# Chunk matrices in other PSUM banks, waits for both banks of a run, and a second block-diagonal tile, in a hybrid RWKV-7 and attention step

## The chip, the cores and the metric

One core of a Trainium2 chip runs one layer of a hybrid decoder as a single program. The metric is the time of one execution on the device, in microseconds (us). Engine names are those of the profile: PE is TensorE's matmul, PEld its weight load, DVE is VectorE, ACT ScalarE, POOL GpSimd, SP the engine that issues most of the DMAs.

## The reference, cut to what matters

One prompt of 4096 tokens and a sample batch of 8 x 8 tokens go through one layer of width 1024. A joint projection feeds eight RWKV heads and eight windowed attention heads; both outputs are gated, projected and added to the input. The part that the change touches is the recurrence of the RWKV heads:

```python
def step(S, xs):
    r_t, w_t, k_t, v_t, a_t, b_t = xs
    Sa = jnp.einsum('bhvk,bhk->bhv', S, a_t)
    S = S * w_t[:, :, None, :] + Sa[..., None] * b_t[:, :, None, :] + v_t[..., None] * k_t[:, :, None, :]
    return S, jnp.einsum('bhvk,bhk->bhv', S, r_t)
```

The kernel doesn't step through tokens. It takes chunks of 64 tokens, for which the recurrence becomes products of 64 x 64 matrices and the inverse of a triangular one.

## The kernel before, in words

The first phase (`phase1`) projects the input and runs the recurrence; the second (`phase_b`) does the attention and the output projections. The prompt is cut into 16 supertiles of 256 tokens (four chunks each); the sample is a 17th, taken second. Per supertile there are four pairs of heads (units); two units make a group, so there are 34 groups.

Stages of the first phase, for the reader of the rows:

- Stage B (`stage_b`): the projections that the recurrence needs, `g_ps` (lines 592 to 594); `shift` copies them out as `k`, `r`, `v` (line 607).
- Stage W (`stage_w`): the other projections, `w_ps` (line 683), with weights streamed from memory; their results go back to memory for the second phase.
- Stage C (`stage_c`, one unit): decay and keys, to the operands `AR` (lines 777 and 798) and `BK` (lines 780 and 801), the bonus `bo` (line 813) and the values `UV` (line 834). Its small products `sum_ps`, `nb_ps`, `b_ps`, `v_ps` and those of the decay (`dec`, lines 643 and 644) use the PSUM pool `pm`, with two banks.
- Stage D (`stage_d`, one group): `tmat` (line 872), once a unit, makes the chunk matrices `t_ps` in two banks, from which six instructions of VectorE take `nf`, `LA` and `Ar` (lines 882 to 885). `m0` (line 893) puts them into the block-diagonal tile `mbd` and makes the first `DG`. Then the inverse is built level by level: `lev1`, four times `levz` and `levd` (two banks at once), a last `levz`, `lastd`, `nz` (the last to read `mbd`), `lastg` and `ng`, which ends in the copy to `G` (line 994). All of these products use the pool `pi`, with two banks, `tmat` too. Between them `tmt` (line 905) transposes `BK` into a bank of `pm`.
- Stage E (`stage_e`, one group): the four chunks one after the other, with the state; from `mean` (line 1120) on the norm of the output, which ends in `yc` (line 1151) and the store to `y_d` by SP (line 1155).

`BK` has three buffers, `AR` five, `UV` and other tiles of a group three (groups), `TM`, `LA` and `Ar` four, `mbd` one. The sum of all of this must fit the eight banks of PSUM and the on-chip memory.

What sets the order: `Timeline` gives every step a due time (a supertile is 4 units of time; stage D of a group starts 1.05 behind stage C of its second unit, stage E 3.1), and the steps are written down in that order. From there a planner fixes, when the program is built, the order of each engine's instructions and the buffer of each tile: it takes the earliest written step among those whose operands and buffers are ready in its model, stages D and E by some instructions ahead of their place. A tile's buffer is whichever of its pool is free first. `together` (line 181) keeps a run of matmuls in its order; with `after` its first one waits for given instructions (`follow`, line 191):

```python
    def together(calls, after=()):
        for i, (out, lhs, rhs) in enumerate(calls):
            ins = pe.matmul(out, lhs, rhs, start=True, stop=True)
            follow(ins, i, after)
```

The way into the second phase: the output of the last group is stored to `y_d` by SP; behind that store on SP stand the loads of `y_d`, of `z_d` and of `w_proj` (lines 1334, 1338, 1314), and TensorE's first output projection is `g_ps` of line 1636. The tiles `prep` and `parts` of the pool `wsl` (two buffers each) hold weights while they are converted and scaled, up to plan time 19; the sample's attention in the second phase uses them again.

Of the kernel before, what the change touches and what calls it, by code (L numbers as in the profile page):

```python
# [137 lines left out]
def hybrid_step(ctx: ExitStack, tc: tile.TileContext, I, O):  # L138
# [240 lines left out]
    def phase1():  # L379
        with ExitStack() as es:  # L380
# [29 lines left out]
            mbd = ck.tile([128, 2, GN * 4, 128], F16, name="mbd")  # L410
            pool.memset(mbd, 0.0)
# [207 lines left out]
            def stage_b(j):  # L619
# [20 lines left out]
                def dec(p):  # L640
# [9 lines left out]
                    act.activation(th, ps, AF.Tanh, scale=0.5, bias=dcol(13 + p))  # L650
                    ta = sb.tile([128, SUP], F32, tag="ta", name="ta")[:, :n]
                    act.activation(ta, ps2, AF.Tanh, scale=0.5, bias=dcol(17 + p))
# [59 lines left out]
            def stage_c(u):  # L712
# [71 lines left out]
                def s5():  # L784
# [8 lines left out]
                    vec.scalar_tensor_tensor(d["k"], d["k"], vcol(V_KK + p), ps[:, :n], ALU.mult, ALU.mult)  # L793
# [10 lines left out]
                def s8():  # L804
# [5 lines left out]
                    for q in range(2):  # L810
                        os_ = slice(64 - 64 * q, 128 - 64 * q)
                        for h in range(min(nch, 2)):
                            act.activation(bo[os_, h::2], pb[64 * h:64 * h + 64, :nh, q], AF.Copy)
# [3 lines left out]
                def s9():  # L817
# [13 lines left out]
                    for q in range(2):  # L831
                        os_ = slice(64 - 64 * q, 128 - 64 * q)
                        for r in range(min(nch, 2)):
                            act.activation(UV[os_, r:nch:2, q, :],
                                                      ps[64 * r:64 * r + 64, :nh, 64 * q:64 * q + 64], AF.Copy)
# [3 lines left out]
            HALF = [slice(0, 64), slice(64, 128)]  # L839

            def stage_d(g):
# [17 lines left out]
                def with_states(e):  # L859
# [7 lines left out]
                    act.activation(AR[:, 2].rearrange("p i (b t) -> p b i t", t=8), ps, AF.Copy)  # L867
# [4 lines left out]
                def tmat(i):  # L872

                    e = ds[i]
                    pss = [pi.tile([128, 4, 128], F32, tag="i", name="t_ps") for q in range(2)]
                    together([(pss[q][:, c, :], e["BK"][qs, c].rearrange("p a t -> p (a t)"),
                               e["AR"][qs, c].rearrange("p a t -> p (a t)"))
                              for c in range(nch) for q, qs in reversed(list(enumerate(HALF)))], e["w_ab"])
                    mk_ = mlrs if smp else mlr
                    for q, qs in enumerate(HALF):  # L880
# [4 lines left out]
                        vec.tensor_tensor(e["Ar"][:, q, :nch], ps[:, :nch, 64:128], bcm(mk_[:, 64:128], nch), ALU.mult)  # L885
# [7 lines left out]
                def m0():  # L893
                    Nf = d["Nf"][:, :nb]
                    M = d["M"] = mbd[:, :, :nb]
                    for q, hs in enumerate(HALF):
                        own = slice(64 * q, 64 * q + 64)
                        act.activation(M[hs, 0, :, own], Nf[hs], AF.Copy)
                        vec.tensor_tensor(M[hs, 1, :, own], Nf[hs], M[hs, 0, :, own], ALU.subtract)
                    DG = sb.tile([128, 2, GN * 4, 64], F16, tag="DG", name="DG", bufs=2)[:, :, :nb]  # L900
# [4 lines left out]
                def tmt(e):  # L905
# [4 lines left out]
                    act.activation(e["TM"][:, :nch].rearrange("p c q f -> p c (q f)"), ps[:, :nch], AF.Copy)  # L910
# [7 lines left out]
                def mmd(ps, part, rhs):  # L918
                    together([(ps[:, m, :], d["M"][:, part, m], rhs(m)) for m in range(nb)])
# [16 lines left out]
                def lev1():  # L936
                    ps = psn()
                    mmd(ps, 0, lambda m: eye16)
                    vec.tensor_tensor(d["DG"][:, 0], ps, bcm(msk[1], nb), ALU.mult)
                L.append((0.6, lev1))  # L940

                def levz(b):
# [3 lines left out]
                    vec.tensor_tensor(Z, ps, bcm(msk[b], nb), ALU.mult)  # L946
                    d["Z"] = Z

                def levd(b):
# [13 lines left out]
                def lastd():  # L963
# [3 lines left out]
                    act.activation(d["D6"], ps, AF.Copy)  # L967
                L.append((0.6, lastd))

                def nz():  # L970
                    ps = psn()
                    for m in range(nb):
                        for part in range(2):
                            follow(pe.matmul(ps[:, m, :], d["M"][:, part, m], d["D6"][:, m], start=part == 0,
                                             stop=part == 1), 2 * m + part)
                    Zf = sb.tile([128, GN * 4, 64], F32, tag="Zf", name="Zf", bufs=1)[:, :nb]
                    vec.tensor_tensor(Zf, ps, bcm(mfin, nb), ALU.mult)
# [3 lines left out]
                def lastg():  # L981
# [3 lines left out]
                    d["w_z"] = [act.activation(d["G6"], ps, AF.Copy)]  # L985
                    act.activation(d["Zh"], d["Zf"], AF.Copy)
# [838 lines left out]
```

## Time and profile before

| | us |
|---|---|
| median of 3 runs | 3227.1 |
| lowest and highest of them | 3219.41 and 3230.64 |
| the profiled execution | 3223.27 |
| span of its instructions | 3221.5 |

| engine | busy us | share of the span | instructions |
|---|---|---|---|
| PE | 2900.6 | 90% | 34028 |
| PEld | 2142.9 | 67% | 34028 |
| DVE | 2062.3 | 64% | 4877 |
| ACT | 1614.7 | 50% | 4353 |
| POOL | 1302.0 | 40% | 3325 |

A share of busy time is a mean over stretches with different limits, so what follows is read by stretch and by group. The first phase runs to some 2205 us, the second starts on TensorE with its projections at 2228 us.

### The profile page before, as it was taken

The page shows a single profiled execution, that of the slowest core. Times are in us where ns is not written, and L with a number is a line of the kernel's source. Part 1 is how long each engine was busy: PE and PEld are TensorE (multiplying, and loading weights), DVE is VectorE, ACT ScalarE, POOL GpSimd, SP SyncE. Part 2 cuts the span into 40 slices and gives each one's busy share as a digit, 9 for nine tenths or more (in the row PEclk, how much of TensorE's full clock was granted, in tenths as well). Part 3 has the DMA queues.
Part 4 walks back from the last instruction along what each step waited for, and adds up shares of the span by engine and source line. Part 5 has one row for each costly group of instructions (what it writes and reads, how often), then busy time and mean ns, then how long its engine had stood idle before and what let it go on. Part 6 is the DMA issues. An engine that isn't in the chain of part 4 may idle for free. (4 is left out here: it accounts for less than half of the span.)

```text
span 3221.5 us, 85488 instructions
## 1 busy us (share of the span) xinstructions
PE 2900.6 (90%) x34028; PEld 2142.9 (67%) x34028; DVE 2062.3 (64%) x4877; ACT 1614.7 (50%) x4353; POOL 1302.0 (40%) x3325
## 2 busy tenths in 40 slices
PE   3789998999999999999999999863899999999899
PEld 2677776788888888888888888751444444444444
DVE  7576776656565666675666665663576766766663
ACT  5573654555555555555555555552344444444331
POOL 3234433534534443544435344451464344434210
PEclk9889999999999999999999999856899999999999
DMA  7774665332332332332332233423576666666643
GB/s 224 238 238 145 223 208 180 101 102 85 96 98 87 103 98 81 102 106 78 91 104 85 87 96 116 137 50 93 117 160 154 148 142 151 159 142 145 138 115 76
DMA packets 470585, 410.69 MB, mean 127 GB/s; under 512 B 313432, under 2 KB 377688, under 8 KB 470168
## 3 DMA queue, kind: packets, MB, share of 16 engines
q1 hardware_dynamic: 451432, 375.39, 43.4%
q10 hardware_dynamic: 18752, 29.83, 2.5%
q8 instruction: 267, 4.37, 0.6%
q14 instruction: 134, 1.10, 0.1%
HBM read 268.95 MB, written 73.69 MB: 106 GB/s over the span
## 5 line engine op out<-in xcount | busy, mean ns | idle before, releaser
L683 PE MATMUL w_ps<-ring,xh 128*128 128x192 f16 (+3 forms) x4224 | 679.2, 262 | 13.4 <-DVE z L693 6.9
L592 PE MATMUL g_ps<-xh,ws 128*128 128x256 f16 (+1 forms) x1768 | 479.2, 275 | 33.2 <-ACT carry L617 25.1
L593 PE MATMUL g_ps<-xl,ws 128*128 128x256 f16 (+1 forms) x1768 | 477.9, 275 | 2.8 <-DVE xl L570 2.8
L594 PE MATMUL g_ps<-xh,ws 128*128 128x256 f16 (+1 forms) x1768 | 477.8, 275 | 0.0
L683 PEld LDWEIGHTS <-xh 128*128 128x128 f16 (+1 forms) x4224 | 387.6, 100 | 56.8 <-issue 15.6
L1636 PE MATMUL g_ps<-ws,th 128*128 128x512 f16 (+1 forms) x792 | 308.9, 396 | 104.5 <-DMA th<-sh 66.7
L683 PE MATMUL w_ps<-ring,xl 128*128 128x192 f16 (+3 forms) x2112 | 387.1, 261 | 0.0
L1637 PE MATMUL g_ps<-ws,th 128*128 128x512 f16 (+1 forms) x792 | 312.1, 394 | 0.0
L1636 PEld LDWEIGHTS <-th 128*128 128x128 f16 (+1 forms) x1056 | 106.3, 101 | 240.3 <-DMA th<-sh 77.8
L593 PEld LDWEIGHTS <-ws 128*128 128x128 f16 x1768 | 176.5, 100 | 57.3 <-issue 35.6
L683 PEld LDWEIGHTS <-xl 128*128 128x128 f16 (+1 forms) x2112 | 198.9, 99 | 16.5 <-issue 1.3
L1056 POOL TENSOR_TENSOR S<-sp,Pe 128x128 f32<-128x128 f32 x128 | 60.2, 470 | 351.9 <-DVE sp L1051 347.2
L592 PEld LDWEIGHTS <-ws 128*128 128x128 f16 x1768 | 177.8, 101 | 30.9 <-issue 3.3
L594 PEld LDWEIGHTS <-ws 128*128 128x128 f16 x1768 | 176.4, 100 | 30.5 <-issue 4.6
L1637 PEld LDWEIGHTS <-th 128*128 128x128 f16 (+1 forms) x1056 | 106.3, 101 | 123.8 <-issue 13.3
L1641 PE MATMUL g_ps<-ws,tl 128*128 128x512 f16 (+1 forms) x792 | 188.1, 379 | 0.0
L1469 ACT ACTIVATE s<-s,nm,ssc 128x128 f32<-128x128 f32 x256 | 123.2, 483 | 126.6 <-DVE nm L1460 126.5
L1641 PEld LDWEIGHTS <-tl 128*128 128x128 f16 (+1 forms) x1056 | 101.8, 98 | 117.5
L211 POOL TENSOR_SCALAR rs_h<-rs_x 128x4 f32<-128x4 f32 (+4 forms) x152 | 36.1, 239 | 284.8 <-DVE rs_x L207 143.1
L946 DVE TENSOR_TENSOR Z<-z_ps,cm 128x512 f16<-128x512 f32 (+1 forms) x164 | 110.6, 674 | 58.1 <-PE z_ps L184 57.3
L780 POOL TENSOR_TENSOR BK<-k,L 64x256 f32<-64x256 f32 (+1 forms) x136 | 100.8, 742 | 99.4 <-PE t_ps L184 68.6
L1479 POOL TENSOR_TENSOR p<-s,p 128x512 f16<-128x512 f32 x64 | 82.3, 1287 | 131.9 <-ACT p L1478 131.7
(382 smaller groups left out, 8075.6 us busy)
## 6 DMA issues: line engine op xcount, KB each, us to landing
ring<-wd SPq DMA_DIRECT2D x132, 512.0 KB
ring<-wd SPq DMA_DIRECT2D x128, 384.0 KB
xtok<-in_x_dram SPq DMA_DIRECT2D x128, 128.0 KB
xf<-in_xT_dram SPq DMA_DIRECT2D x64, 256.0 KB
z_d<-z ACTq DMA_DIRECT2D x64, 256.0 KB
zz<-z_d SPq DMA_DIRECT2D x32, 512.0 KB
x<-in_x_dram SPq DMA_DIRECT2D x32, 512.0 KB
out_y_dram<-gt SPq DMA_DIRECT2D x64, 256.0 KB
```

What stands on the lines that cost most here:

```text
L592: pe.matmul(ps, wh[:, cs], xh, start=k == 0, stop=False)
L593: pe.matmul(ps, wh[:, cs], xl, start=False, stop=False)
L594: LAST["g"] = pe.matmul(ps, wl[:, cs], xh, start=False, stop=k == KT - 1)
L683: pe.matmul(st["ps"][:, a:a + c], x, w[:, k % 2, i, a:a + c], start=k == 0 and x is xh and i == 0 and a == 0, stop=k == KT - 1 and i == 1 ...
L780: d["w_ab"].append(pool.tensor_tensor(bk[1 - q][qs], c_seg(d["k2"])[qs], c_seg(d["L"])[qs], ALU.mult))
L946: vec.tensor_tensor(Z, ps, bcm(msk[b], nb), ALU.mult)
L1056: pool.tensor_tensor(sn, t, bc(P[:, :, c], 64), ALU.mult)
L1469: act.activation(s[:, b], s[:, b], AF.Exp, scale=ssc[:, 0:1], bias=nm[:, b:b + 1], accum_out=den[:, b:b + 1])
L1479: pool.tensor_tensor(p16[:, 1], s, p16[:, 0], ALU.subtract)
L1636: pe.matmul(st["ps"], h, wh, start=k == 0, stop=False)
L1637: pe.matmul(st["ps"], h, wl, start=False, stop=False)
L1641: pe.matmul(st["ps"], l, wh, start=False, stop=k == nk - 1)
```

## The change

Four things are done. The chunk matrices `t_ps` go from the pool `pi` to the pool `pm`, and their runs start with the first half of the partitions rather than the second. Two lists, `READ` and `READM`, gather the instructions that read banks of `pi` and of `pm` last, in the order in which the steps are written down; the first matmul of `tmat` and of `levd` now also waits for the last two of its list. The block-diagonal tile is held as a list of pairs, and from the supertile with index 6 on there is a second pair, in the two buffers of `prep`; groups take the pairs in turn. From then on the first `DG` of a group lies in a buffer of `parts`. The cut diff (where a reader is only added to a list, one such line stands for the others):

```diff
-            mbd = ck.tile([128, 2, GN * 4, 128], F16, name="mbd")
-            pool.memset(mbd, 0.0)
+            mb0 = ck.tile([128, 2, GN * 4, 128], F16, name="mbd")
+            pool.memset(mb0, 0.0)
+            mbd = [[mb0[:, i] for i in range(2)]]
+
+            def more_mbd():
+
+                t = [wsl.tile([128, 512], F32, tag="prep", name="mbd", bufs=2).bitcast(F16).rearrange(
+                    "p (m t) -> p m t", t=128) for i in range(2)]
+                for x in t:
+                    pool.memset(x, 0.0)
+                mbd.append(t)
...
+            LATER = 6
+            READM = []
...
+                            last = act.activation(UV[os_, r:nch:2, q, :],
+                                                  ps[64 * r:64 * r + 64, :nh, 64 * q:64 * q + 64], AF.Copy)
+                    READM.append(last)
...
-                    pss = [pi.tile([128, 4, 128], F32, tag="i", name="t_ps") for q in range(2)]
+                    pss = [pm.tile([128, 4, 128], F32, tag="m", name="t_ps") for q in range(2)]
                     together([(pss[q][:, c, :], e["BK"][qs, c].rearrange("p a t -> p (a t)"),
                                e["AR"][qs, c].rearrange("p a t -> p (a t)"))
-                              for c in range(nch) for q, qs in reversed(list(enumerate(HALF)))], e["w_ab"])
+                              for c in range(nch) for q, qs in enumerate(HALF)], e["w_ab"] + READM[-2:])
...
-                    M = d["M"] = mbd[:, :, :nb]
+                    if j == LATER and len(mbd) == 1:
+                        more_mbd()
+                    M = d["M"] = [x[:, :nb] for x in mbd[g % len(mbd)]]
...
-                    DG = sb.tile([128, 2, GN * 4, 64], F16, tag="DG", name="DG", bufs=2)[:, :, :nb]
+                    if len(mbd) > 1:
+                        DG = wsl.tile([128, 512], F32, tag="parts", name="DG", bufs=2).bitcast(F16).rearrange(
+                            "p (a m t) -> p a m t", a=2, t=64)
+                    else:
+                        DG = sb.tile([128, 2, GN * 4, 64], F16, tag="DG", name="DG", bufs=2)[:, :, :nb]
...
-                    together(alternate(mm(p1, Z, DG[:, 1]), mm(p0, DG[:, 1], Z)))
-                    act.activation(DN[:, 0], p0, AF.Copy)
-                    act.activation(DN[:, 1], p1, AF.Copy)
+                    together(alternate(mm(p1, Z, DG[:, 1]), mm(p0, DG[:, 1], Z)), READ[-2:])
+                    READ.append(act.activation(DN[:, 0], p0, AF.Copy))
+                    READ.append(act.activation(DN[:, 1], p1, AF.Copy))
```

`READM` holds the two copies of `dec`, the readers of `nb_ps` (`s5`), `b_ps` (`s8`), `v_ps` (`s9`) and `bk_ps` (`tmt`), and of `tmat` the two products that make `Ar`. `READ` holds the readers of all the level products.

## Rows read from the trace of the kernel before

**Rows 1.** The page: TensorE's busy time, share, instructions, and its granted clock in tenths.
```profile
PE 2900.6 (90%) x34028; PEld 2142.9 (67%) x34028; DVE 2062.3 (64%) x4877; ACT 1614.7 (50%) x4353; POOL 1302.0 (40%) x3325
...
PEclk9889999999999999999999999856899999999999
```

**Rows 2.** Stretches: from:to, length, busy by engine (instructions), TensorE's clock, DMA share, GB/s.
```profile
core 0: us, PE busy (x) PEld busy (x) DVE busy (x) ACT busy (x) POOL busy (x), PEclk, DMA share, GB/s
300.00:900.00 600.00, 559.62 (x7458) 471.52 (x7456) 394.22 (x931) 324.32 (x891) 253.73 (x681) 0.97 0.46 144
900.00:2000.00 1100.00, 1076.05 (x15704) 921.25 (x15704) 698.56 (x1574) 608.34 (x1636) 477.50 (x1286) 1.00 0.31 94
2076.00:2204.00 128.00, 69.09 (x1120) 56.43 (x1115) 73.74 (x175) 53.15 (x149) 67.08 (x173) 0.55 0.22 44
2204.00:2228.00 24.00, 0.11 (x1) 0.14 (x2) 10.73 (x21) 3.60 (x5) 3.64 (x3) 0.50 0.86 223
```

**Rows 3.** In order of time, around 1127 us: start, length, engine, line [idle before].
```profile
1127.22 0.60 ACT L994 ACTIVATE G<-z_ps 128x512 f32<-128x512 f32 x1 [1.30 <-PE z_ps L926]
...
1127.10 0.48 PE L184 MATMUL t_ps<-AR,BK 64*128 64x128 f32 x2
...
1130.43 1.16 PE L184 MATMUL t_ps<-AR,BK 64*128 64x128 f32 x14
...
1131.41 0.45 DVE L882 COPY_PREDICATED nf<-cm,t_ps 64x256 f32<-64x256 uint32 x1 [0.33 <-PE t_ps L184]
```

**Rows 4.** Line 994 from 1200 to 2015 us: count, durations, first and last start.
```profile
L994 ACT ACTIVATE G<-z_ps x14: 578/597/600, 1249.8 to 2013.8; 128x512 f32<-128x512 f32 x14
```

**Rows 5.** In order of time: the operands and the first reader, last group but one.
```profile
1987.71 0.47 ACT L607 ACTIVATE k<-g_ps,dv 128x256 f32<-128x256 f32 x1
...
2022.61 0.85 DVE L801 TENSOR_TENSOR BK<-ta,L 64x256 f32<-64x256 f32 x2
...
2044.66 1.56 POOL L777 TENSOR_TENSOR AR<-r,P 128x256 f32<-128x256 f32 x2 [5.67 <-PE y_ps L184]
...
2051.25 1.12 ACT L834 ACTIVATE UV<-v_ps 64x128 f32<-64x128 f32 x4
...
2071.88 0.45 DVE L882 COPY_PREDICATED nf<-cm,t_ps 64x256 f32<-64x256 uint32 x1
```

**Rows 6.** In order of time: the same of the program's second group.
```profile
190.29 0.85 DVE L801 TENSOR_TENSOR BK<-ta,L 64x256 f32<-64x256 f32 x2
...
191.49 0.45 DVE L882 COPY_PREDICATED nf<-cm,t_ps 64x256 f32<-64x256 uint32 x1
```

**Rows 7.** In order of time: the last group, to the second phase's first projection.
```profile
2032.80 0.48 ACT L607 ACTIVATE k<-g_ps,dv 128x256 f32<-128x256 f32 x1 [2.64 <-DMA z_d<-z]
...
2086.95 0.98 DVE L801 TENSOR_TENSOR BK<-ta,L 64x256 f32<-64x256 f32 x2
...
2102.16 1.12 ACT L834 ACTIVATE UV<-v_ps 64x128 f32<-64x128 f32 x4
...
2132.54 0.45 DVE L882 COPY_PREDICATED nf<-cm,t_ps 64x256 f32<-64x256 uint32 x1
...
2172.61 0.60 ACT L994 ACTIVATE G<-z_ps 128x512 f32<-128x512 f32 x1 [1.88 <-PE z_ps L926]
...
2191.04 0.69 DVE L1120 TENSOR_REDUCE mean<-yc 128x8 f32<-128x512 f32 x1
...
2204.60 2.56 SPq L1155 DMA_DIRECT2D y_d<-yc  x4
...
2227.89 0.59 PE L1636 MATMUL g_ps<-ws,th 128*128 128x512 f16 x1 [37.57 <-DMA wt<-in_w_proj_dram]
```

**Rows 8.** TensorE's waits, 600 to 2000 us: line, releaser: us, times, longest.
```profile
PE z_ps L926 <- DVE Zl L987: 4.6, 4, 2.5
...
PE dg_ps L184 <- DVE Z L946: 3.8, 2, 3.0
PE z_ps L184 <- ACT DG L954: 2.2, 3, 0.9
...
PE bk_ps L908 <- ACT TM L910: 1.1, 1, 1.1
```

More of the change, by code (lines that the diff above doesn't have):

```diff
@@ L812, in s8 @@
                         for h in range(min(nch, 2)):
-                            act.activation(bo[os_, h::2], pb[64 * h:64 * h + 64, :nh, q], AF.Copy)
+                            last = act.activation(bo[os_, h::2], pb[64 * h:64 * h + 64, :nh, q], AF.Copy)
+                    READM.append(last)
                     d["bo"] = bo
@@ L839, in phase1 @@
             HALF = [slice(0, 64), slice(64, 128)]
+            READ = []
             def stage_d(g):
@@ L866, in with_states @@
                             pe.matmul(ps[qs, b], sv[qs], AR[qs, 0, :, 8 * b:8 * b + 8], start=True, stop=True)
[L867 removed]
+                    READ.append(act.activation(AR[:, 2].rearrange("p i (b t) -> p b i t", t=8), ps, AF.Copy))
                 if smp:
@@ L918, in mmd @@
                 def mmd(ps, part, rhs):
-                    together([(ps[:, m, :], d["M"][:, part, m], rhs(m)) for m in range(nb)])
+                    together([(ps[:, m, :], d["M"][part][:, m], rhs(m)) for m in range(nb)])
                 def mm2(ps, lhs1, lhs2, rhs, after):
@@ L938, in lev1 @@
                     mmd(ps, 0, lambda m: eye16)
-                    vec.tensor_tensor(d["DG"][:, 0], ps, bcm(msk[1], nb), ALU.mult)
+                    READ.append(vec.tensor_tensor(d["DG"][:, 0], ps, bcm(msk[1], nb), ALU.mult))
                 L.append((0.6, lev1))
@@ L945, in levz @@
                     Z = f16t("Z", 3)
-                    vec.tensor_tensor(Z, ps, bcm(msk[b], nb), ALU.mult)
+                    READ.append(vec.tensor_tensor(Z, ps, bcm(msk[b], nb), ALU.mult))
                     d["Z"] = Z
@@ L966, in lastd @@
                     d["D6"] = f16t("D6", 1)
-                    act.activation(d["D6"], ps, AF.Copy)
+                    READ.append(act.activation(d["D6"], ps, AF.Copy))
                 L.append((0.6, lastd))
@@ L973, in nz @@
                         for part in range(2):
-                            follow(pe.matmul(ps[:, m, :], d["M"][:, part, m], d["D6"][:, m], start=part == 0,
+                            follow(pe.matmul(ps[:, m, :], d["M"][part][:, m], d["D6"][:, m], start=part == 0,
                                              stop=part == 1), 2 * m + part)
                     Zf = sb.tile([128, GN * 4, 64], F32, tag="Zf", name="Zf", bufs=1)[:, :nb]
-                    vec.tensor_tensor(Zf, ps, bcm(mfin, nb), ALU.mult)
+                    READ.append(vec.tensor_tensor(Zf, ps, bcm(mfin, nb), ALU.mult))
                     d["Zf"] = Zf
@@ L985, in lastg @@
                     d["w_z"] = [act.activation(d["G6"], ps, AF.Copy)]
+                    READ.append(d["w_z"][0])
                     act.activation(d["Zh"], d["Zf"], AF.Copy)
@@ L993, in ng @@
                     G = sb.tile([128, GN * 4, 64], F32, tag="G", name="G", bufs=2)[:, :nb]
-                    act.activation(G, ps, AF.Copy)
+                    READ.append(act.activation(G, ps, AF.Copy))
                     d["G"] = G
```

18 lines of the change are left out of this document (9 added, 9 removed).

## The prediction

> **What bounds the kernel now.** I read the page first, then the table of stretches, then TensorE's waits, then single groups in order of time, and last the way out of the first phase. On the page TensorE is busy 90% of the span, and its granted clock has one trough, in slices 26 to 28 [rows 1]. The table of stretches says where the other 10% lie: from 900 to 2000 us TensorE is busy 1076 of 1100 us at a clock of 1.00; from 300 to 900 us it is idle for 40 us; and from 2076 to 2228 us, the way from the first phase to the second, it is busy 69 of 152 us at a clock of about 0.55, where half of full speed (1.2 of 2.4 GHz) is 0.50 [rows 2]. So in the long middle nothing but TensorE's idle 24 us can be won, and a change that takes no column off TensorE must earn its time at the passage.
>
> The reader should not stop there, because TensorE is full of work that can be done at any time (the streamed products `w_ps`), and that hides a second bound. Look at one group of stage D (two pairs of heads, four chunks each). Its last product's copy, `G`, starts at 1127.22. The first two products of the next group's chunk matrices, `t_ps`, stand at 1127.10: they took the one bank of `pi` that was free. The other 14 follow at 1130.43, after that copy gave the second bank back, and the first reader runs at 1131.41 [rows 3]. The next group thus begins when the last one ends, and only then. From 1249.8 to 2013.8 there are 14 copies of `G`, so a group comes every 58.8 us [rows 4]: stage D runs one group at a time, without a pause.
>
> What it delays is seen at the end. For the last group but one `BK` is written at 2022.61 to 2023.46 while its first `nf` runs at 2071.88, 48 us later; GpSimd's `AR` of the same group waits 5.67 us for a product of stage E two groups back, and the copies to `UV` come at 2051 [rows 5]. In the second group of the program, where nothing is behind, `BK` ends at 191.14 and `nf` starts at 191.49 [rows 6]. So stage D is late by tens of us, and this lateness comes due when no projections are left to cover it: for the last group `BK` ends at 2087.93, the `UV` copies at 2103.28, `nf` starts at 2132.54, `G` at 2172.61, the mean at 2191.04, the output is stored at 2204.60, and TensorE's next product, held by the loads queued behind that store on SP, starts at 2227.89 after 37.57 us of nothing [rows 7].
>
> **The change part by part.** *Chunk matrices in `pm`.* The same 32 products and 12 readers a group; no duration changes, and the order of the two halves within the run has no price that I can see. What goes is the wait for both `pi` banks. Next late is what the products read: `BK`, and the operand of the new wait (below). The last group stood from 2103.28 to 2132.54, 29 us, after all of these were there [rows 7]; I leave 2 us for queues and take **-27**, with bounds 0 and -44.6 (from the end of `BK`).
>
> *Stage C is set free.* Its buffers (three `BK`, five `AR`, three `UV`) are given back by stages D and E. The last unit took from the end of its `k` copy at 2033.28 to the end of `BK` at 2087.93, 54.7 us; the unit two before took from 1988.18 to 2023.46, 35.3 us [rows 5, 7]. I take the difference, **-19**, bounds 0 and -19.4.
>
> *Work pulled forward.* If stage D is 42 us less late (2071.88 down to about 2030, a few us behind `BK` [rows 5]), TensorE has done 42/58.8 of a group more when the last projections end, and they end later by that. From 2076 to 2204 it was busy 69.09 us at a clock of 0.55 [rows 2], some 38 us at full clock, mostly for the levels and chunks of a little over two groups; so about 19 us a group at most, and **+13**, bounds 0 and +19.
>
> *Idle time before the passage.* The waits of stage D's own products from 600 to 2000 us are 4.6, 3.8 and 2.2 us [rows 8]; some of these vanish where two groups can be mixed, and some of the 40 us before 900 [rows 2] too. I take **-10**, bounds 0 and -20.
>
> *The second phase starts sooner.* Its attention for the first tiles used the passage as cover. TensorE's 24 us from the last store to its first product (2204 to 2228) [rows 2] stay as they are; for attention that is not ready I add **+5**, bounds 0 and +24.
>
> *The new waits.* `levd` waits for the last two readers in `READ`: these are the copy that wrote its own `DG` and the product that wrote its own `Z`, so it waits for nothing that it does not read. Nothing, whatever hides it. The second `tmat` waits for the readers of the first, which held both banks anyway. The first `tmat` waits for the last copies to `bo` and `UV` of the unit traced before it; they ended at 2103.28 where `BK` ended at 2087.93, 15 us later [rows 7], so once stage D has no lag this is what it waits for; that is why the first term starts at 2103.28. Behind it on TensorE stand projections, which the planner puts ahead of a run that isn't ready; who waits for it is this group's six readers on VectorE.
>
> *Second block-diagonal tile and the new `DG`.* From the seventh supertile on a group's `m0` need not wait for the last group's `nz`. Two memsets of 128x1024 on GpSimd, once, and no instruction more per group. The buffers it takes are used before by the weight scales alone, which the plan ends at 19 where the seventh supertile starts at 28, and the sample's attention, which wants them next, comes after the last group. Even with one tile the next `m0` could start behind `nz`, with three steps of the group before still to come; and TensorE's own load, 0.978 of 58.8, asks for 57.5 us a group in any case [rows 2, 4]. I cost this part at **0**, bounds 0 and -10 at the last group, whose levels could run beside those of the group before.
>
> The sum is -27 -19 +13 -10 +5 = **-38 us**. The profiled execution took 3223.3 us (span 3221.5), so 3185; the median shown is 3.8 us above it, so **3189 us**.
>
> A page speaks against this sum. The Trainium skill, "Perfetto Trace Analysis", section "Identifying the Most-Contended Engine", says to take the engine with the highest occupancy as the bottleneck and to optimize that one first (and to judge TensorE by the busy share of its weight loads). Here the weight loads are busy 921 of 1100 us in the middle [rows 2], more than VectorE's 699: by that rule a change that gives TensorE nothing less to do gives nothing, which is the third rival below. The trace agrees for the middle and not for the passage.
>
> **The rivals.** *Half of it (chance 0.16).* The lag goes, but stage C does not get faster, since `AR` is still held by stage E two groups back (the 5.67 us wait [rows 5] speaks for it; that stage E itself would end earlier speaks against). Then -27 +13 -5 +5 = -14: **3213 us**.
>
> *More (0.12).* The last two groups' levels mix through two tiles, and the idle time before 2000 falls by its bound: -38 -10 -10 -17 (from the 29.3 us of the first term to its bound of 44.6) = -75: **3152 us**. For it: TensorE is idle for 83 us in the passage [rows 2]. Against: the chain from `nf` to the mean took 58.5 us even with the engines nearly empty [rows 7].
>
> *No change (0.13).* TensorE was full, the lag is only moved, and the second phase's own start (loads and attention) takes the place of the wait: **3227 us**, give or take 9. For it: the 97.8% in the middle. Against: the 37.57 us in which TensorE waits for loads that stand behind the last store on SP [rows 7].
>
> *Slower (0.09).* The `pm` banks become the narrow place. A run of `tmat` holds both for its 16 products (14 in 1.16 us) and six readers of some 0.45 us, 1.3 + 2.7 = 4.0 us [rows 3], twice a group, and the small products of stage C that stand in TensorE's queue in an order fixed beforehand then stop the projections behind them. Today such a stop costs 1.1 us (`bk_ps`) and happened once from 600 to 2000 us [rows 8]. At one such stop in each of 34 groups the 38 us are gone; that is the point from which it decides. Two stops a group cost 75 us: **3264 us**.
>
> **How the numbers follow.** The forecast, 3189 with a range of its own from 3165 to 3208, gets 0.50. A measurement of this kernel can tell about 0.3%, or 9.7 us, from no change. Faster by more: forecast, half of it and more, 0.50 + 0.16 + 0.12 = 0.78. Same 0.13, slower 0.09. The range from 3145 to 3226 leaves out the slower case, some 0.05 of no change and some 0.04 of the case "more".
>
> **What would show it.** In the profile after: the first `nf` of a group within some 10 us of the group's `UV` copies, in the middle and at the last group; the spacing of the `G` copies shorter than 58.8 us or, if TensorE sets it, 57 to 58; no GpSimd wait for `t_ps`; TensorE's busy share in the middle at 98% or above; the first product of the second phase near 2190 instead of 2228. Wrong in the lag: `nf` still some 30 us after `UV`. Wrong in stage C: `k` to `BK` of the last unit still near 55 us. Slower would show as waits of `sum_ps`, `nb_ps`, `b_ps`, `v_ps` or `bk_ps` for readers in `pm`, over 1 us a group. The prediction fails altogether if the first product of the second phase moves and the end does not: then the second phase, and not its start, sets the time.

## The result, and the profile after

The changed kernel took 3207.5 us in the median (3205.6 to 3208.0), 0.9942 of the kernel before, with an interval from 0.9924 to 0.9960; timed twice more beside other kernels it came to 0.9929 (0.9906 to 0.9952) and 0.9935 (0.9915 to 0.9955). So it is faster by 0.6%, some 20 us. The forecast of 38 us had the sign and nearly twice the size. The profiled execution has a span of 3205.8 us against 3221.5.

First the stretches, with the columns of [rows 2]; the row of the first 300 us of the kernel before was not among those, so it stands here first, alone.

```profile
0.00:300.00 300.00, 215.88 (x2594) 174.73 (x2594) 199.87 (x539) 173.41 (x549) 99.83 (x333) 0.91 0.67 210
```

The changed kernel:

```profile
0.00:300.00 300.00, 198.26 (x2256) 162.55 (x2256) 180.90 (x487) 163.59 (x513) 88.07 (x289) 0.86 0.66 203
300.00:900.00 600.00, 560.85 (x7618) 469.97 (x7616) 400.39 (x956) 326.48 (x905) 261.36 (x718) 0.98 0.46 145
900.00:2000.00 1100.00, 1074.15 (x15912) 926.05 (x15912) 711.84 (x1612) 612.20 (x1657) 493.08 (x1305) 1.00 0.31 95
2076.00:2192.00 116.00, 62.88 (x1038) 52.81 (x1034) 69.10 (x156) 48.21 (x134) 61.43 (x159) 0.61 0.30 68
2192.00:2215.00 23.00, 0.13 (x1) 0.14 (x2) 10.62 (x21) 3.60 (x5) 3.73 (x3) 0.50 0.87 233
```

The middle is as full as before. The passage is 13 us shorter (116 and 23 us, where [rows 2] have 128 and 24). New is the first row: TensorE is busy 17.6 us less in the first 300 us, and the sum has no term for that.

The last group, step by step as in [rows 7], in order of time:

```profile
2053.59 0.47 ACT L618 ACTIVATE k<-g_ps,dv 128x256 f32<-128x256 f32 x1
...
2079.15 0.84 DVE L812 TENSOR_TENSOR BK<-ta,L 64x256 f32<-64x256 f32 x2
...
2081.05 1.12 ACT L846 ACTIVATE UV<-v_ps 64x128 f32<-64x128 f32 x4
...
2084.67 0.43 DVE L896 COPY_PREDICATED nf<-cm,t_ps 64x256 f32<-64x256 uint32 x1
...
2153.10 0.60 ACT L1016 ACTIVATE G<-z_ps 128x512 f32<-128x512 f32 x1 [0.98 <-PE z_ps L947]
...
2165.56 0.28 ACT L1082 ACTIVATE yc<-y_ps 128x128 f32<-128x128 f32 x1 [4.86 <-DMA y_d<-yc]
...
2179.11 0.69 DVE L1142 TENSOR_REDUCE mean<-yc 128x8 f32<-128x512 f32 x1
...
2192.67 2.56 SPq L1177 DMA_DIRECT2D y_d<-yc  x4
...
2214.87 0.59 PE L1658 MATMUL g_ps<-ws,th 128*128 128x512 f16 x1 [36.47 <-DMA wt<-in_w_proj_dram]
```

Each step against the same step of [rows 7], beside the term that the sum had for it (us):

| from, to | before | after | difference | forecast |
|---|---|---|---|---|
| start to the last `k` copy | 2033.3 | 2054.1 | +20.8 | +13 -10 |
| to the end of `BK` | 54.7 | 25.9 | -28.8 | -19 |
| to the end of the `UV` copies | 15.4 | 2.2 | -13.2 | 0 |
| to the first `nf` | 29.3 | 2.5 | -26.8 | -27 |
| to the end of the last `G` | 40.7 | 69.0 | +28.3 | 0 |
| to the mean | 17.8 | 25.4 | +7.6 | 0 |
| to the store | 13.6 | 13.6 | 0 | 0 |
| to the second phase's first product | 23.3 | 22.2 | -1.1 | 0 |
| to the end of the span | 993.6 | 990.9 | -2.7 | +5 |
| sum | | | -15.9 | -38 |

The lag is gone: `nf` follows the `UV` copies by 2.5 us, as forecast. Two other steps are far from the sum. The last `k` copy is 17.8 us later than it said, and the last group's levels and chunks, from `nf` to the mean, take 36 us longer. The experiments go to these two, and to which part of the change does what.

### The profile page after: what moved, and what is told of

It reads as the page before. It is cut to its first block, busy times and chain, and to the rows that moved or that the text cites. A ratio compares the mean times of both kernels' runs of the same rounds, so it can differ in the third digit from the quotient of the medians.

```text
span 3205.8 us, 85349 instructions
## 1 busy us (share of the span) xinstructions
PE 2884.0 (90%) x34028; PEld 2132.4 (67%) x34028; DVE 2058.9 (64%) x4877; ACT 1608.9 (50%) x4353; POOL 1317.0 (41%) x3327
## 5 line engine op out<-in xcount | busy, mean ns | idle before, releaser
L694 PE MATMUL w_ps<-ring,xl 128*128 128x192 f16 (+3 forms) x2112 | 396.2, 263 | 0.0
L791 POOL TENSOR_TENSOR BK<-k,L 64x256 f32<-64x256 f32 (+1 forms) x136 | 114.1, 839 | 120.4 <-PE bk_ps L929 82.5
```

The costliest lines, as they stand in the source:

```text
L694: pe.matmul(st["ps"][:, a:a + c], x, w[:, k % 2, i, a:a + c], start=k == 0 and x is xh and i == 0 and a == 0, stop=k == KT - 1 and i == 1 ...
L791: d["w_ab"].append(pool.tensor_tensor(bk[1 - q][qs], c_seg(d["k2"])[qs], c_seg(d["L"])[qs], ALU.mult))
```

## The experiments

All runs but those with an output buffer of its own for the last group, which come further down, in one view. The second column is the ratio to the kernel before with its interval; then come readings of each one's profiled execution: TensorE's idle time in the first 300 us, the last `k` copy, the time from there to the last store, and the second phase's first product (us).

| kernel | ratio | idle to 300 | last `k` | `k` to store | first product |
|---|---|---|---|---|---|
| before | 1 | 84.1 | 2033.3 | 171.3 | 2227.9 |
| the change | 0.9942 (0.9924 to 0.9960) | 101.7 | 2054.1 | 138.5 | 2214.9 |
| again (e5) | 0.9929 (0.9906 to 0.9952) | 98.4 | 2047.1 | 139.3 | 2208.4 |
| again (e18) | 0.9935 (0.9915 to 0.9955) | 99.8 | 2042.1 | 138.3 | 2203.9 |
| e1 one tile | 0.9992 (0.9973 to 1.001) | 96.0 | 2049.8 | 149.1 | 2221.2 |
| e2 tile alone | 0.9990 (0.9973 to 1.0008) | 87.5 | 2026.1 | 174.0 | 2222.7 |
| e3 four supertiles as before | 0.9938 (0.9919 to 0.9957) | 87.4 | 2046.2 | 142.0 | 2210.9 |
| e4 no first wait | 1.0052 (1.0031 to 1.0074) | 98.3 | 2076.8 | 138.4 | 2238.0 |
| e6 last D first | 0.9924 (0.9903 to 0.9944) | 99.1 | 2041.7 | 140.3 | 2204.2 |
| e8 tile last | 0.9914 (0.9891 to 0.9937) | 102.2 | 2047.7 | 139.0 | 2210.0 |
| e9 last two D first | 0.9928 (0.9908 to 0.9948) | 99.8 | 2046.7 | 142.1 | 2211.6 |
| e10 last group in `pm` | 0.9932 (0.9915 to 0.9948) | 102.0 | 2046.0 | 139.3 | 2207.3 |
| e11 first supertile as before | 0.9915 (0.9895 to 0.9935) | 85.6 | 2030.1 | 143.3 | 2194.5 |
| e12 and the sample | 0.9946 (0.9926 to 0.9965) | 87.8 | 2040.5 | 143.4 | 2206.3 |
| e13 `pi` up to the tenth | 0.9940 (0.9925 to 0.9954) | 84.7 | 2053.9 | 141.0 | 2216.3 |

Executions of one program differ by several us in the last `k` copy (the three of the change: 2054.1, 2047.1, 2042.1), much less in the step from there to the store (138.3 to 139.3), and the time from the second phase's first product to the end was 986 to 999 us in the executions of this table, without order. So a step is better read against its neighbour than against the clock on the wall, and one span proves nothing below some 10 us.

**The parts alone.** One tile to the end:

```
-            LATER = 6
+            LATER = 99
```

> The chunk matrices in the small products' banks, and one block-diagonal tile to the end. Theory (the tile is worth nothing, as the sum had it): the time of the changed kernel, 3207 us within 5; the last group's G ends near 2154 as there. Rival A (the two tiles let the last two groups mix, and that is part of the 12 us by which the last store came earlier): 3213 to 3219. Rival B (the mixing is what stretched the last group from 35.4 to 64.1 us between m0 and G): 3190 to 3200, with m0 to G of the last group back near 40 us.

And the chunk matrices back in `pi`, without the waits of `READM`, with the second tile kept (the order of the halves goes back with them):

```
-                    pss = [pm.tile([128, 4, 128], F32, tag="m", name="t_ps") for q in range(2)]
+                    pss = [pi.tile([128, 4, 128], F32, tag="i", name="t_ps") for q in range(2)]
```

> Only the second block-diagonal tile and the waits of the levels; the chunk matrices stay in the two banks of the stage, without the new waits. Theory (the tile is worth nothing, since a group cannot begin before the last one has ended): 3227 us within 5, nf 45 to 53 us behind BK in the late groups, as before, and TensorE idle for about 84 us in the first 300 us. Rival A of the run with one tile: 3215 to 3221.

Each part alone gives nothing that can be measured, and both together give 0.6%. That the tile alone gives nothing was expected (`nf` 44.3 us behind `BK` at the last group: it cannot begin anyway). That the banks alone give nothing was not: from the last `k` copy to the store they win 22 us (171.3 to 149.1), and up to that copy they lose 16.5. With the second tile the store is another 10 us nearer. That run also asks for the tile where it should act, at the last two groups only:

```
-            LATER = 6
+            LATER = NSUP - 1
```

> The changed kernel with the second block-diagonal tile only for the last supertile, whose two groups are the last two of the program. With one tile throughout the time was 0.9992 of the kernel before, with two from the seventh supertile on 0.9942. Theory (the tile is worth something only where the last group meets the one before it: with one tile the last group's m0 began 12.0 us behind its first nf, with two 4.9): 0.994, the time of the changed kernel within 5 us. Rival (it is worth something in the steady middle, by the mixing of groups): 0.999, the time of the run with one tile. Rival (the difference between the two runs lay in the order drawn up anew and not in the tile): anything, with m0 to G of the last group unlike that of the changed kernel.

It gives all that the change gives (0.9914; 139.0 us from `k` to store): through the whole middle the second tile is worth nothing. How much it is worth at the end is not settled. The kernel with one tile also runs in another rhythm in the middle (`m0` to `G` 56, 46, 53 and 48 us in turn, where the change has 50 and 48), so the planner drew up another order. One tile in the middle does not bring that rhythm by itself, for e8 has one there too and runs as the change does (50 and 48). Kernels with two tiles in that rhythm (e3, e11, e12) have 142 to 143.4 us from `k` to store; by an estimate from these, some 6 of the 10 us are the tile and 4 the order.

**The start.** What the first group's runs of chunk matrices did, in order of time; before:

```profile
85.66 2.08 PE L184 MATMUL t_ps<-AR,BK 64*128 64x128 f32 x16 [0.17 <-DVE BK L801]
...
120.82 1.16 PE L184 MATMUL t_ps<-AR,BK 64*128 64x128 f32 x16
```

and after:

```profile
126.32 0.49 PE L184 MATMUL t_ps<-AR,BK 64*128 64x128 f32 x2
...
127.82 1.16 PE L184 MATMUL t_ps<-AR,BK 64*128 64x128 f32 x14
...
169.67 0.50 PE L659 MATMUL d_ps<-t,wlh 64*128 64x256 f32 x2
...
172.63 0.50 PE L659 MATMUL a_ps<-t,wlh 64*128 64x256 f32 x2 [1.66 <-DVE sw_t L237]
...
174.20 0.46 ACT L663 ACTIVATE ta<-a_ps,dv 128x256 f32<-128x256 f32 x1
...
174.81 2.08 PE L184 MATMUL t_ps<-AR,BK 64*128 64x128 f32 x16 [1.56 <-ACT t L640]
```

The first run is 41 us later, the second 54 us, and between them no instruction writes or reads a tile in `pm` for 35 us (134.3 to 169.7). The second run stands in the fixed order behind `d_ps` and `a_ps` of the supertile's last unit, which are late in both kernels (the last of that unit's decay is read at 170.2 us before and 174.7 after). I had asked whether chunk matrices would hold up the small products; here the small products hold up the chunk matrices. Is it the banks, or the new wait at a run's start? Two kernels tell: the first four supertiles and the sample in `pi` without the wait, and all in `pm` without the wait at the group's first run.

```
+                    old = smp or j < 4
-                    pss = [pm.tile([128, 4, 128], F32, tag="m", name="t_ps") for q in range(2)]
+                    pss = [(pi if old else pm).tile([128, 4, 128], F32, tag="i" if old else "m", name="t_ps")
+                           for q in range(2)]
...
+                             e["w_ab"] + ([] if old else READM[-2:]))
```

> The changed kernel, but the first four supertiles and the sample keep the chunk matrices in the two banks of the stage, without the new waits. In the changed kernel TensorE is idle for 101.7 us of the first 300, against 84.1 before, and the projections stay some 20 us late to the end. Theory (the new place of the chunk matrices costs that at the start, and it is never made good): the first 300 us show 80 to 90 us of idle time, the last k copy comes near 2036 instead of 2054, and the time is 3190 us within 6. Rival (the end is set by the chain of the last two groups, so an earlier last projection only waits longer): idle time as in the theory, but 3202 to 3208 us. Rival (the start is late for another reason, the order drawn up anew): idle time still near 100 us and 3207.

```
-                              for c in range(nch) for q, qs in enumerate(HALF)], e["w_ab"] + READM[-2:])
+                              for c in range(nch) for q, qs in enumerate(HALF)], e["w_ab"] + (READM[-2:] if i else []))
```

> The changed kernel, but the first of a group's two runs of chunk matrices no longer waits for the last readers of the small products; the second still waits for the readers of the first. Theory (it is this wait, which ties the first unit's run to the UV copies of the second, that put the first nf of the program from 90.5 to 131.7 us and made the start late): the first nf is back at 90 to 100 us, idle time of the first 300 us 80 to 90, and 3190 us within 6. Rival (it is the banks: the runs and the small products of stage C stand in each other's way): nf earlier, but idle time near 100 us and 3203 to 3210. Rival (the wait protected the projections): TensorE stands inside the runs, 3215 or more.

The wait of the first run is not what makes the start late: without it the first `nf` is still at 128.9 us (131.7 with it), the idle time at 98.3, and the kernel is slower than the kernel before. That wait is useful: without it a product of `t_ps` takes 97 ns in the middle (57.39 us for 592 from 900 to 2000), with it 83 (51.56 for 624). But e4 leaves the second run its wait. In the written order the `dec` of the supertile's last unit stands between the two runs, so the second run waits for the two copies of that very `dec`, not for the readers of the first run as the prediction had it; it starts 0.15 us behind the second of them (174.66 and 174.81; the row names ScalarE's next instruction, `t`, which the run does not read). For the second run, then, banks and wait ask for the same, and no run parts them. With the old banks at the start the idle time is back at 87.4 us. Over all runs, those further down included, the split is clean: 84 to 88 us wherever the first supertile is in `pi`, 93 to 102 wherever it is in `pm`. But the time did not follow: the last `k` copy came at 2046.2, not 2036. So I narrowed it to the first supertile, then to that and the sample (`old = j == 0`, `old = smp or j == 0`):

> The changed kernel, but only the two groups of the first supertile keep the chunk matrices in the two banks of the stage. In the changed kernel the second run of the first group stands 41 us behind the first (133.9 to 174.8), in the order of the small products' banks behind d_ps and a_ps of the last unit of the supertile; in the kernel before it ran at 120.8. Theory (that is the start's loss): k of the thirteenth unit near 410 to 415 as before (429 to 434 in the changed kernel), the last k copy 10 to 17 us earlier than there (2047 to 2054), 3188 to 3196 us. Rival (as with four supertiles and the sample in the old banks, where the start was regained and then lost again by the last unit): last k copy 2044 to 2050, 3200 to 3207.

> As the run before, with the sample's groups, which come second, in the old banks too. The same theory and rival; between the two runs it is seen whether it is the first supertile or the sample where the delay arises. 3188 to 3196, or 3200 to 3207 by the rival.

Both regain the start (end of the thirteenth `k` copy at 415.2 and 406.6, before 409.6, after 434.0). It is the first supertile then, not the sample. The first of them has the last `k` copy at 2030.1 and 3198 us, the second 2040.5 and 3208: the same start, 10 us apart at its end, and both in the other rhythm of the order, whose way from `k` to store is 4 to 5 us longer. That `pm` with its waits in the first supertile costs some 13 us of idle time at the start (the mean of the one kind of run against that of the other) is shown; that its recovery reaches the end is not.

**When the lag must go.** `pi` up to the tenth supertile (`old = smp or j < 10`):

> The chunk matrices move to the small products' banks only from the eleventh supertile on; the lag of stage D (45 to 53 us) builds up before that as in the kernel before, and stage D makes it good at about 8 us a group (50 us of its own against 58 of TensorE). Theory (what the lag costs is paid at the passage alone, so it is enough to be rid of it by then): the time of the changed kernel or better by the start that it keeps, 3190 to 3205 us, the last k copy at 2040 to 2050, the last store near 2180 to 2190. Rival (the new place makes every group's runs of products shorter, and half of the gain lies in the middle): 3207 to 3216.

0.9940: the lag of 45 to 53 us, kept to the 22nd group, costs nothing, and it is enough to be rid of it by the passage. This run also shows the work pulled forward, which I had at 13 us, without the late start. Up to the 43rd unit its `k` copies are those of the kernel before (1320.0 and 1320.5); then stage D catches up (`nf` behind `BK` from 53.1 to 11.6 us), and the 55th comes 10.9 us later (1684.5 and 1673.6), the 61st 8.2 and the last one 20.6. And it holds both kinds of run in one execution, busy time for `t_ps` alone (products in brackets):

```profile
600.00:1400.00 800.00, 44.80 (x416) 33.34 (x416) 62.70 (x156) 0.99 0.30 94
1500.00:2000.00 500.00, 23.70 (x288) 18.89 (x288) 44.68 (x108) 0.99 0.31 95
```

That is 107.7 ns a product in `pi` and 82.3 in `pm`, or 0.81 us a group of 32 products, which I had at "no duration changes". (The trace lists sixteen products a run where the program has eight, two for each.) The difference lies in breaks. One run of each kind, first in `pi`, then in `pm`:

```profile
817.45 0.48 PE L184 MATMUL t_ps<-AR,BK 64*128 64x128 f32 x2
821.61 1.16 PE L184 MATMUL t_ps<-AR,BK 64*128 64x128 f32 x14
...
1637.32 1.16 PE L184 MATMUL t_ps<-AR,BK 64*128 64x128 f32 x16 [0.26 <-ACT UV L846]
```

In `pi` all 26 runs of the first stretch break behind the first two, and 8 of them once more (1.64 us busy with one break, 1.91 with two); in `pm` 10 of the 18 runs of the second go through whole, in 1.16 us (the whole run at 174.81 above took 2.08, at a granted clock of 0.50). Over the 24 groups from the 13th to the 61st unit 0.81 us are 19 us, and that fits what the change regains there: its `k` copies are 24.4 us late at the 13th unit and 13.4 at the 61st, though by e13 8.2 us of work were pulled forward by then.

**The passage.** In the change the last group's first level product stands directly behind the last one of the group before:

```profile
2103.14 0.27 PE L947 MATMUL z_ps<-G,Zl 64*64 64x64 f16 x2
2103.35 0.61 PE L184 MATMUL z_ps<-eye,mbd 128*128 128x64 f16 x8
```

while its `m0` copies began at 2089.58. From one `G` to the next it takes 49.6 us. Three runs push at this chain: stage D of the last group, or of the last two, ahead of stage E in the planner's priority, and stage D of the last group in the banks of `pm`.

```
-                        tl.stage(t + LAG_D * f, 1.9 * f, lambda u=u: stage_d(u // GN), PD)
+                        tl.stage(t + LAG_D * f, 1.9 * f, lambda u=u: stage_d(u // GN),
+                                 prio(800) if u // GN == 2 * NSUP - 1 else PD)
```

> The changed kernel, but the last group's stage D goes ahead of stage E in the planner's priority (800 in place of 200, where stage E has 500). Theory (the last group's 64.1 us from m0 to G, against 35.4 before, are its turns behind the steps of the group before it, D up to 2104 and E up to 2137): m0 to G 45 to 55 us, the last store 8 to 15 us earlier, 3190 to 3198 us. Rival (the wait is for the banks of the level products, which the group before holds until its own G at 2104, and the chain from there takes 50 us by itself): G near 2150, time within 4 us of the changed kernel. Rival (stage E of the group before is pushed back by as much and becomes the last): G 10 us earlier, the last store not, same time.

(For both groups: `if j == NSUP - 1`.)

> As the run before this one, but both groups of the last supertile go ahead of stage E. Theory: G of the last group but one also comes earlier (2104 less 5 to 8), and with it the last group's; 3184 to 3194 us. Rival (D of the last but one is bound by its own chain and by TensorE): same as the run with the last group alone. Rival (stage E two groups back is late, it holds AR and so the last unit of stage C): k to BK of the last unit longer than 26 us, and 3205 to 3215.

```
+                end = g == 2 * NSUP - 1
                 def psn(name="z_ps"):
-                    return pi.tile([128, GN * 4, 64], F32, tag="i", name=name)[:, :nb]
+                    po, tag = (pm, "m") if end else (pi, "i")
+                    return po.tile([128, GN * 4, 64], F32, tag=tag, name=name)[:, :nb]
...
+                    if end:
+                        DN = wsl.tile([128, 512], F32, tag="parts", name="DG", bufs=2).bitcast(F16).rearrange(
+                            "p (a m t) -> p a m t", a=2, t=64)
```

> The changed kernel, but the very last group of stage D takes its level products into the small products' two banks (free by then, stage C has ended) and its new DG tiles from the weight scales' buffers, so that it shares no bank with the group before it. Theory (in the changed kernel the last group stands behind the group before it: its first level product runs at 2103.35, directly behind that group's last at 2103.14, though its m0 copies began at 2089.6): the first level product follows m0 within 8 us, G of the last group comes 8 to 15 us earlier against the last k copy, and the last store 5 to 12 us; 3192 to 3200 us. Rival (the two chains then take turns on TensorE, VectorE and ScalarE, and what one gains the other loses): G of the last earlier by 5 or less, store within 4 us, 3202 to 3208 us. Rival (stage E of the last two groups is the end): G earlier by 8 to 15 and store within 4.

All three bring the last `G` nearer (e6 by less than it was to), and none brings the store nearer. The last `G` comes 94.7, 91.8 and 87.5 us behind the last `k` copy, where the change has 99.6; the store comes 140.3, 142.1 and 139.3 us behind it, where the change has 138.5. Something behind `G` holds. In the last of them ScalarE, in order of time:

```profile
2132.85 0.59 ACT L1026 ACTIVATE G<-z_ps 128x512 f32<-128x512 f32 x1
...
2142.93 0.28 ACT L1063 ACTIVATE us<-u_ps 128x128 f32<-128x128 f32 x1 [1.60 <-PE u_ps L184]
2158.25 0.28 ACT L1092 ACTIVATE yc<-y_ps 128x128 f32<-128x128 f32 x1 [15.05 <-DMA y_d<-yc]
```

`yc` has one buffer. The last group's stage E may not write its first output before the group before it has been normed and stored (SP issued that store at 2153.98). The row was there in the change too, with 4.86 us; the earlier the last `G`, the longer it is (10.53 in e6). So the last group got an output buffer of its own, one of `BK`'s, free by then:

```
-                    d["yc"] = sb.tile([128, GN * 4, 64], F32, tag="yc", name="yc", bufs=1)[:, :nb]
+                    if g == 2 * NSUP - 1:
+                        d["yc"] = sb.tile([128, 4, 2, CH], F32, tag="BK", name="yc", bufs=3).rearrange(
+                            "p c a t -> p (c a) t")
+                    else: ...
```

in the change, in e10 (`pm` for the last group), in e11 (first supertile as before), and in both at once:

> The changed kernel, but the last group's output yc has a buffer of its own (one of BK's, which stage C no longer needs). Theory (the last group's stage E waits for the store of the group before it: ScalarE's 4.86 us there): the last store 4 to 6 us nearer to the last k copy, 133 to 135 instead of 138.5, and 3198 to 3203 us. Rival (stage E of the last group is late by its turns beside attention): 137 or more, no change.

> The same buffer, with the last group of stage D in the small products' banks. Theory (with these banks the last G came 12 us earlier and ScalarE then waited 15.05 us for the one yc): the last store 122 to 128 us behind the last k copy instead of 139.3, and 3188 to 3196 us. Rival (the two stages E then stand in each other's way through their other single buffers, us and sp): 130 or more, 3196 to 3203.

> The buffer for yc, with the first supertile's chunk matrices in the old banks. Theory (start and passage are separate and add up): 5 us less than the run with the first supertile alone, whose ratio was 0.9915: 0.990, 3188 to 3198 us. Rival (the regained start was a chance of that set): 0.992 to 0.994.

> First supertile in the old banks, last group of stage D in the small products' banks, and a yc of its own for the last group. Theory (three separate stops, each shown by its own wait): last k copy 2030 to 2042, last store 122 to 128 behind it, 0.985 to 0.988 of the kernel before, 3176 to 3188 us. Rival (what the passage gains, the second phase gives back as attention loses its cover): first product of the second phase early by 15 to 20 us, but the span from there to the end longer than 995 us, and 3192 or more.

| kernel | ratio | last `k` | `k` to store | first product |
|---|---|---|---|---|
| e14 own `yc` | 0.9905 (0.9886 to 0.9923) | 2041.1 | 135.1 | 2198.8 |
| e15 with e10 | 0.9918 (0.9891 to 0.9944) | 2049.4 | 127.5 | 2199.4 |
| e16 with e11 | 0.9910 (0.9894 to 0.9926) | 2035.1 | 137.4 | 2194.6 |
| e17 all three | 0.9900 (0.9877 to 0.9923) | 2036.3 | 137.8 | 2197.4 |

The wait on `y_d<-yc` is gone, and the step to the store is shorter by most of what it cost: 138.5 to 135.1 us in the change (4.86 us of wait), 139.3 to 127.5 with e10 (15.05). So the single `yc` was what came late next. The three gains don't add up: e17 has e11's rhythm, its last group takes 56.8 us from `m0` to `G` where e15 takes 52.7, and its store is no nearer to `k` than e16's. In time all four lie near 0.991. Whether that is below the change was asked once more, side by side:

> The changed kernel again, as the measure for the next run: 0.993 to 0.994 of the kernel before.

> The changed kernel with a buffer of its own for the last group's output, again. Theory (4 us at the passage reach the end): 3 to 6 us below the changed kernel of this set. Rival (the 9 us seen between the sets were the sets): within 2 us of it.

0.9935 (0.9915 to 0.9955) for the change, 0.9923 (0.9902 to 0.9944) for the own `yc`: medians of 3199.4 and 3199.1 us. The trace has the gain again (133.4 us from `k` to store, 138.3 in the change beside it); the time does not show it. The 11 us between the medians of the earlier sets (3204.9 and 3193.9) are not found again.

## Why the prediction was wrong in size

Point by point, with the steps of the sum.

- **What bounds the kernel** held. The middle stayed full (1074 of 1100 us), the lag was paid at the passage, and e13 shows it was paid there alone. The rule of the Trainium skill ("Perfetto Trace Analysis", section "Identifying the Most-Contended Engine") to take the engine of the highest occupancy first says less than the prediction read into it: not that nothing else pays. Here the second phase's first product came 13 us sooner while no column was taken off TensorE.
- **Chunk matrices in `pm`, -27** held to the us (-26.8), and the start of `nf` 2.5 us behind `UV` with it. What I missed is that `UV` itself came 13.2 us nearer to `BK`.
- **Stage C is set free, -19**: the mechanism was right and it was worth more, -28.8, beyond my bound of -19.4. I took two units of one trace as the ends, and neither was free of the lag.
- **Work pulled forward, +13** was too small at the place where the sum puts it: by the last `k` copy e13, which keeps the start, is 20.6 us later than the kernel before. In the change the shorter runs hide it, up to the same copy (stretch, length, busy time and products of TensorE in all, then of `t_ps` alone; before first, then after):

```profile
0.00:2033.27 2033.27, 1884.82 (x26190) 0.98 0.41 127
0.00:2033.27 2033.27, 107.05 (x976) 0.98 0.41 127
...
0.00:2054.07 2054.07, 1886.79 (x26590) 0.97 0.41 126
0.00:2054.07 2054.07, 86.26 (x992) 0.97 0.41 126
```

  400 more products and only 2.0 us more of work, since `t_ps` takes 20.8 us less. So the 20.8 us of the first step are 18.8 of idle time and 2.0 of work.
- **Idle time before the passage, -10** is the step that failed. It came out at +18.8 (TensorE's idle time up to the last `k` copy, 148.5 before and 167.3 after; 163.5 and 163.0 in the change's two other executions), 17.6 of it in the first 300 us. I gave bounds of 0 and -20 and excluded a loss without a reason. I looked at the new order of the banks only from 600 us on, where stage D has slack; in the first supertile the small products of the last unit are late, and there chunk matrices stood free of them in `pi` and now stand behind them. e3, e11 and e12 show that it is `pm` with its waits, e4 that it is not the wait of the first run; banks and wait of the second run are not parted.
- **Nothing late next behind `nf`** is the second. I let the last group run its 58.5 us from `nf` to the mean as in [rows 7], where the group before was nearly out of its way. Brought forward by 48 us it meets that group: its levels wait for `pi` until 2103, its copies for `yc` until 2165, and the way takes 94.4 us. That gives back 36 us of a gain of 69 (28.8, 13.2 and 26.8). I listed the buffers of stage C that would come free earlier and not those that the last two groups share. These two are only a part of it: with banks and a `yc` of its own (e15) the way is still 83.3 us. TensorE's busy time and products from `nf` to the mean, before, after and in e15:

```profile
2132.54:2191.04 58.50, 35.25 (x610) 0.59 0.15 26
...
2084.67:2179.11 94.44, 54.93 (x887) 0.59 0.36 82
...
2080.03:2163.31 83.28, 55.21 (x887) 0.59 0.40 93
```

  So 11 of the 36 us are shown to be the shared banks and `yc`. For the other 25 the cause is argued: TensorE has 20 us more to do in between (levels of the group before, streamed products, attention), and no run takes that out.
- **No duration changes** was wrong in the kernel's favour: 0.8 us a group, by fewer breaks, shown in e13 within one execution.
- **The second tile, 0** held for the middle (e8, e2) and not at the last group, where 6 to 10 us lie within the bounds of 0 and -10 that I gave.
- **Luck.** Against the sum stand 29 us of idle time and 36 us of the last group; for it came 43 us that it did not have: stage C 9.8, `UV` 13.2, the shorter runs against the work pulled forward 11, the second phase 8.8. That the sign and half of the size came out is in good part luck.
- **The rivals.** "Half of it" came nearest in time, for another reason than it gave: stage C did get faster. "Slower" had the right place and the wrong direction. Waits for readers in `pm` stay small (`d_ps` for `Ar` 6.4 us in all from 600 to 2000), and it is the chunk matrices that wait. (The -17 in "More" is 15.3 by the two numbers beside it; its chance does not hang on that.)
- Of the signs to look for, `nf` comes 1.3 and 9.1 us in turn behind its group's `UV` copies in the middle, within the 10 us said. The copies of `G` are 58.2 us apart (15 of them from 1070.0 to 1885.2), but only in the mean: 69 and 47 us in turn. GpSimd no longer waits for `t_ps`, as said; it now waits for the next thing that gives `BK` back, 64.5 us for `bk_ps` from 600 to 2000 where it was 63.5 for `t_ps`. TensorE's share in the middle, 97.6%, missed the 98% by a little. The first product at 2214.9 instead of 2190 is the sum's error again.

## What to carry to other kernels

When a stage that ran late is pulled forward, ask at its new place what it shares with the work that it now overtakes: every single-buffered tile and every bank, up to the last store. And when products move from a pool of their own to a shared one, look at the start and the end of the program as well as at the middle: what is free of charge under slack is paid where one unit is late. Two parts of a change may each measure as nothing and still be worth something together, so test them together before one is thrown out.

## What I had not expected of the hardware

By the profile's rows a run of small products that breaks keeps TensorE busy for longer, besides what it waits: 1.16 us for the sixteen in one piece, 0.48 and 1.16 us for two and fourteen. The fourteen alone take as long as all sixteen, with other work of TensorE between the two pieces. And one program gave its last `k` copy at 2054.1, 2047.1 and 2042.1 us in three executions; the granted clock in the first 300 us was 0.86, 0.88 and 0.89, and 0.98 in each from 300 to 900 us. At the thirteenth `k` copy they stood at 434.0, 429.1 and 426.6 us already, so much of the scatter is there before 450 us; what makes it was not tried.
